# Half of the up-projection groups with tokens as rows, and all head pairs turned by DMA, in a two-layer decoder trunk

## The chip, the core and the metric

The kernel runs on one core of one Trainium2 chip. A core has TensorE (PE in the profile; PEld is its loading of the stationary operand), VectorE (DVE), ScalarE (ACT), GpSimd (POOL) and SyncE (SP), whose queue here issues nearly all DMAs. The metric is the device time of one execution in microseconds. Three runs of the kernel before took 555.38, 555.40 and 556.26 us, a median of 555.4.

## The reference

`x` is 256 tokens of 1024 features in fp32. There are two layers. Layer 0 mixes tokens with a gated MLP in chunks of 128 tokens, layer 1 with causal attention of 16 heads of 64 (with 256 tokens there is only the query's own block) and a relative-position bias. Each mixer is followed by a gated MLP with a causal depthwise convolution, and each of the four sub-layers ends in `x = LayerNorm(alpha * x + f(x))`:

```python
def conv_ffn(x, w_up, conv_w, conv_b, w_down):
    h = x @ w_up                                  # 1024 -> 2 x 2816
    hp = jnp.pad(h, ((0, 0), (CONV_WIDTH - 1, 0), (0, 0)))
    hc = conv_b
    for j in range(CONV_WIDTH):                   # width 3, along the tokens
        hc = hc + conv_w[j] * hp[:, j:j + S]
    g, val = jnp.split(hc, 2, axis=-1)
    return (jax.nn.gelu(g) * val) @ w_down

s = q k^T / 8 + bias[bucket(distance)]            # attention, causal
o = softmax(s) v
```

## The kernel before, in words

**Precision.** Every large matmul is done in three: weights and activations are each split into a high part (rounded to fp32r) and a low part (the rest), and high x high, high x low and low x high are added in PSUM. Weights come as chunks of 128 x 2048 fp32 (1 MB) into one of two `raw` buffers by SP's queue (L407). ScalarE writes the high part `whi` (L383), VectorE the low part `wlo` (L389), each 128 x 1024 half into the next of ten buffers. So a chunk is loaded and split up to two and a half groups ahead of its use.

**Column form of the up stages.** `conv_up` makes 22 tiles of 128 gate features and 22 of 128 value features. A group takes two of each, 512 features in all, from two chunks. In the column form (`cols_apart`) a block of weights is the stationary operand and the tokens stream: per feature tile and block of 128 inputs one matmul of 512 columns (high weights against high and low tokens of all 256) and one of 256 (low weights against high tokens). All high parts of a group come first, then all low ones. The result has features as rows, as the convolution along the tokens wants it. Behind the first group of a stage (the head, below) ten such groups follow, counted from 0; the even ones use the four single banks (`bank`), the odd ones the two double ones (`twos`).

**Row form.** The first group of each up stage (the head) is made otherwise: the tokens are the stationary operand and 512 features of weights stream, three matmuls of 512 columns per block of inputs and half of the tokens. The result has tokens as rows and has to be turned. ScalarE copies the bank into two planes of 16-bit halves (`over`, L963), a DMA transposes them (`xbar`, L426, on SP's queue), and copies put the halves together again (`join`, L971 on VectorE, L973 on ScalarE).

**Gate.** `gate` convolves the four tiles (ScalarE one step, VectorE two each, L393), applies the GELU, multiplies and splits the product into the two parts that the down stage reads from `rr`. The down stage (`project_out`) is in row form, goes through the 22 feature tiles in order and takes the last six behind all others.

**Attention.** `project` makes queries and keys of a pair of heads in column form, `scores` the scores of two pairs (four heads) into both double banks. `softmax` reduces on VectorE (L1104), takes the exponential on ScalarE (L383) and normalises on VectorE (L1112). The probabilities must be turned before they meet the values. For pairs 0 to 5 this is done by DMA (`turn_apart`: copies into planes L1127, transpose L426, joins L1130); for pairs 6 and 7 by 12 transposes on TensorE through the identity (L377) and four copies out of PSUM on ScalarE (`take`). `apply` multiplies with the values; `values` makes the second half of the values behind the last scores.

**What sets the order.** All operations are recorded with a duration that the author estimates; a list scheduler (`Plan`) then places them, engine by engine, by due times worked back from TensorE's stream, and the order on each engine is fixed when the program is built. Matmuls of the main stream keep their recorded order; transposes, scores and applications are fillers that go in where the plan has them ready. The plan is made, VectorE's work just ahead of the first normalisation is held behind it, and the plan is made again.

Of the kernel before, what the change touches and what calls it, by code (L numbers as in the profile page):

```python
# [19 lines left out]
P = 128  # L20
# [34 lines left out]
PASSES = 1  # L55
# [3 lines left out]
LAST_TURN = (6,)  # L59
APART_BY = ['act/dve', 'act/dve', 'act/dve', 'act/dve', 'act/dve', 'act/dve', 'act/dve', 'act/dve']  # L60
JOINED_BY = ['dve/act', 'dve/act', 'dve/act', 'dve/act', 'dve/act', 'dve/act', 'dve/act', 'dve/act']
BY_XBAR = (0, 1, 2, 3, 4, 5)
# [29 lines left out]
class Plan:  # L92
# [44 lines left out]
    def emit(self):  # L137
        ops = self.ops
        for o in ops:
            for b in o.bufs:  # L140
                for q in b.prev:
                    o.deps.update(x for x in q.ops if x is not o)
            assert all(d.i < o.i for d in o.deps), "a group waits for one recorded after it"

        self.dues()
        order = self.schedule()
        first = [o for o in order if o.first]
        for o in order:
            if o.eng == "dve" and not o.first and first[0].start - LEAD <= o.start < first[0].start:
                o.after = first[-1]  # L150
        for _ in range(PASSES):
            self.dues()
            order = self.schedule()

        done, held = set(), []
        for o in order:
            held.append(o)
            while True:
                x = next((x for x in held if x.deps <= done and (x.after is None or x.after in done)), None)
                if x is None:  # L160
                    break
                held.remove(x)
                x.emit()
                done.add(x)
        assert not held
# [104 lines left out]
def trunk_kernel(ctx: ExitStack, tc: tile.TileContext, a: dict, out: bass.AP):  # L270
# [88 lines left out]
    def mms(seq, r, w, fill=False, into=None, ready=False, share=1, turn=0.0):  # L359

        ns = 0.0
        for o, l, x, _, _ in seq:
            n = flat(x)
            ns += (max(n, 240) + 32) / 2.4 * 0.96 if l.dtype == F32R else (218.0 if n <= P else n / 0.6 + 5)
# [400 lines left out]
    def project_out(name, nk, at, xold, li, rows_i):  # L765
# [7 lines left out]
        if name == "b_o":  # L773
            free[1:3] = free[2:0:-1]
# [145 lines left out]
    def conv_up(layer, h, l):  # L920
# [39 lines left out]
        def over(t, b, to):  # L960
            a = planes.new()
            av = a.ap.bitcast(U16)
            plan.op("act", 1040, lambda: nc.scalar.copy(av.rearrange("p (h x) -> p h x", h=2), halves(b.ap)), [b], [a])  # L963
            xbar(to.ap.bitcast(U16).rearrange("p (g t q) -> p t g q", t=NT, q=P)[:, t], av, [a], [(to, [t])])

        def join(to, o, j, by):
# [3 lines left out]
            if by == "dve":  # L970
                dve(440, lambda: nc.vector.tensor_copy(to_, src), [(to, range(NT))], part)  # L971
            else:
                plan.op("act", 770, lambda: nc.scalar.copy(to_, src), [(to, range(NT))], part)  # L973
# [16 lines left out]
        for i in range(2):  # L990
            o = oring.new()
            gate(i, [join(across, o, 2 * i + j, "act" if j in BY_ACT else "dve") for j in range(2)], psum=False)
        for n, i in enumerate(range(2, FT, 2)):
            subs = [sub(name, i + x, j) for x in range(2) for j in range(2)]
# [6 lines left out]
            for x in range(2):  # L1001
                spent(name, i + x)
                gate(i + x, joined(bs[x]) if n % 2 else joined_apart(bs[2 * x:2 * x + 2]), psum=False)
        return lambda k, t: (av[:, k, t * P:(t + 1) * P], lv[:, k, t * P:(t + 1) * P], [(ah, [k]), (al, [k])])


    def moba(h, l, scr):
# [108 lines left out]
        def by(engines, first, j, fn, r, w):  # L1116
            e = engines.split("/")[j % len(engines.split("/"))]
            ns = {"act": (860, 1080), "dve": (590, 620), "pool": (1050, 1050)}[e][not first]
# [59 lines left out]
        for i in range(PAIRS):  # L1178
# [4 lines left out]
            if i in TURNS_BEHIND:  # L1183
                turn(TURNS_BEHIND[i], end)
        visit(PAIRS - 2)(end)
        values(1, [bank(True) for _ in range(NT)], [(t, range(KT)) for t in range(NT)])
# [38 lines left out]
def _layout(i):  # L1225
# [32 lines left out]
    for n in range(DEPTH):  # L1258
        pairs = paired(up[n][:, :FFN], up[n][:, FFN:])
        head = pairs[:2].reshape(2, P, 2, KT, P).transpose(1, 3, 0, 2, 4)  # L1260
        pairs[:2] = head.reshape(P, 2, CH).transpose(1, 0, 2)
# [33 lines left out]
```

## Time and profile before

| | |
|---|---|
| profiled execution | 555.37 us, span 553.6 us, granted clock 0.997 |
| busy: PE, PEld, DVE, ACT | 546.0, 467.9, 477.8, 381.4 us |
| layer 0: mixer until about 88 us, up stage to 199, down stage 199 to 272 (by the chain) | |
| layer 1: attention from 272 and its output projection, until about 376; up stage 376 to 487, down stage from 487 | |
| DMA | 114.37 MB, mean 207 GB/s, 58.6% of 16 engines for the main queue |

The stages overlap where a normalisation lets the next one begin. A row of the chain of waits gives start, length, engine, tile, line and count of instructions; a row of the order of time gives start, busy time, engine, line, operation, tiles and shape; a row of groups ends in busy time, mean nanoseconds of one, and the idle time before them.

### The profile page before, as it was taken

Reading aid. Unit: us, or ns where it says so; the run is one execution under the profiler, and the core shown is the slowest. Engines: PE = TensorE matmul, PEld = TensorE weight load, DVE = VectorE, ACT = ScalarE, POOL = GpSimd, SP = SyncE. Lnnn points to the kernel's source line nnn. Section 1 sums busy time; section 2 is a strip of 40 time slices with the busy share of each in tenths; the row PEclk is TensorE's granted clock in tenths of the full one; section 3 lists DMA queues with packets and bytes.
Section 4 is the critical chain, followed back from the end, with each engine's and each line's share of the span. In section 5 each row is a group of like instructions: output and inputs, shape, how many; then the busy total and the mean of one; then the engine's idle time right before and its main releaser. Section 6 shows DMA issues by size and latency. Waiting matters only on the chain.

```text
span 553.6 us, 8263 instructions
## 1 busy us (share of the span) xinstructions
PE 546.0 (99%) x2990; PEld 467.9 (85%) x2990; DVE 477.8 (86%) x914; ACT 381.4 (69%) x708; POOL 16.5 (3%) x22
## 2 busy tenths in 40 slices
PE   9999999999999999999999999999999999999995
PEld 6889888988898888888888887888888988888885
DVE  5898989899999999568978998789899999899837
ACT  6657567977677777355668998487975777768711
POOL 0200210000000000001000000000000000000001
PEclk9999999999999999999999999999999999999998
DMA  8988418764555276753566886729744654465502
GB/s 322 418 307 326 160 76 200 299 224 153 190 206 194 95 247 227 287 206 146 176 220 144 197 244 235 286 94 281 272 157 167 218 220 153 153 255 207 223 0 76
DMA packets 33200, 114.37 MB, mean 207 GB/s; under 512 B 15926, under 2 KB 19208, under 8 KB 21000
## 3 DMA queue, kind: packets, MB, share of 16 engines
q1 hardware_dynamic: 32872, 113.59, 58.6%
q8 instruction: 23, 0.38, 0.3%
q10 hardware_dynamic: 288, 0.26, 0.1%
q14 instruction: 17, 0.14, 0.1%
HBM read 109.36 MB, written 1.07 MB: 199 GB/s over the span
## 4 chain that ended last, share of the span: by engine, by line
PE 92%; DVE 5%; DMA 2%; issue 0%; ACT 0%; POOL 0%; DVEq 0%; ACTq 0%
PE bank L371 60%; PE twos L371 30%; DVE wlo L389 2%; DMA raw<-in_a_out 1%; PE bank L377 1%; DVE x L393 1%; DMA ff<-in_head 1%; DVE stat L628 0%; DVE ff L389 0%; DVE ff L393 0%; DVE rr L389 0%; PE twos L377 0%; ACT whi L383 0%; POOL stat L634 0%; DVE stat L668 0%
## 5 line engine op out<-in xcount | busy, mean ns | idle before, releaser
L389 DVE TENSOR_TENSOR wlo<-raw,whi 128x1024 fp32r<-128x1024 f32 (+1 forms) x202 | 219.4, 1115 | 16.1 <-ACT whi L383 15.6
L383 ACT ACTIVATE whi<-raw 128x1024 fp32r<-128x1024 f32 (+1 forms) x202 | 186.1, 966 | 43.7 <-DMA raw<-in_f_up 15.3
L371 PE MATMUL bank<-whi,rr 128*128 128x512 f32 x432 | 134.7, 390 | 0.0
L371 PE MATMUL bank<-xt,whi 128*128 128x512 f32 x512 | 120.1, 390 | 0.0
L371 PEld LDWEIGHTS bank<-xt,whi 128*128 128x128 f32 x512 | 95.0, 188 | 19.0
L371 PEld LDWEIGHTS bank<-whi,rr 128*128 128x128 f32 x432 | 81.1, 188 | 17.3 <-issue 0.3
L371 PE MATMUL bank<-wlo,rr 128*128 128x512 f32 x216 | 84.1, 389 | 0.0
L393 DVE SCALAR_TENSOR_TENSOR ff<-ff,convc 128x255 f32<-128x255 f32 (+1 forms) x176 | 76.6, 477 | 7.1 <-ACT ff L383 6.7
L371 PE MATMUL twos<-xt,whi 128*128 128x512 f32 x320 | 74.4, 390 | 0.0
L371 PEld LDWEIGHTS twos<-xt,whi 128*128 128x128 f32 x320 | 59.4, 188 | 11.9
L371 PEld LDWEIGHTS bank<-xt,wlo 128*128 128x128 f32 x512 | 63.9, 191 | 1.8 <-issue 0.2
L371 PE MATMUL bank<-xt,wlo 128*128 128x256 f32 x512 | 65.3, 284 | 0.0
L383 ACT ACTIVATE ff<-ff,convc 128x256 f32<-128x256 f32 x88 | 48.6, 591 | 4.2 <-DVE ff L389 4.0
L371 PEld LDWEIGHTS bank<-wlo,rr 128*128 128x128 f32 x216 | 40.6, 188 | 8.1
L383 ACT ACTIVATE ff<-bank 128x256 f32<-128x256 f32 (+1 forms) x60 | 23.2, 391 | 29.7 <-PE bank L371 23.3
L371 PEld LDWEIGHTS twos<-xt,wlo 128*128 128x128 f32 x320 | 39.7, 192 | 0.8
L371 PE MATMUL twos<-xt,wlo 128*128 128x256 f32 x320 | 40.0, 283 | 0.0
L383 ACT ACTIVATE ff<-bank,lncol 128x128 f32<-128x128 f32 x48 | 18.8, 460 | 19.5 <-PE bank L377 19.4
L371 PE MATMUL twos<-whi,xt 128*128 128x512 f32 x96 | 31.4, 395 | 0.0
L371 PE MATMUL bank<-whi,xt 128*128 128x512 f32 x96 | 29.1, 393 | 0.4 <-DVE whi L414 0.4
L383 ACT ACTIVATE ff<-ff 128x256 f32<-128x256 f32 x52 | 19.9, 410 | 10.4 <-DVE rr L389 8.6
L383 ACT ACTIVATE ff<-twos 128x512 f32<-128x512 f32 (+1 forms) x24 | 13.4, 574 | 18.9 <-PE twos L371 17.2
(118 smaller groups left out, 532.1 us busy)
## 6 DMA issues: line engine op xcount, KB each, us to landing
raw<-in_f_up SPq DMA_DIRECT2D x44, 1024.0 KB, 4.8
raw<-in_f_dn SPq DMA_DIRECT2D x22, 1024.0 KB, 4.8
raw<-in_b_qk SPq DMA_DIRECT2D x8, 1024.0 KB, 4.8
lnrow<-in_lnrow SPq DMA_DIRECT2D x5, 1024.0 KB, 7.1
raw<-in_a_out SPq DMA_DIRECT2D x4, 1024.0 KB, 6.3
raw<-in_b_v SPq DMA_DIRECT2D x4, 1024.0 KB, 4.8
raw<-in_b_o SPq DMA_DIRECT2D x4, 1024.0 KB, 4.9
raw<-in_a_u SPq DMA_DIRECT2D x3, 1024.0 KB, 8.4
```

The source lines that it names most:

```text
L371: nc.tensor.matmul(o, l, x, start=start, stop=stop)
L377: nc.tensor.transpose(o, x, ident.ap)
L383: return plan.op("act", ns, lambda: nc.scalar.activation(o, x, func, **kw), r, w, table=table)
L389: return dve(70 + 1.04 * flat(x), lambda: nc.vector.tensor_tensor(o, x, y, op=op), r, w)
L393: lambda: nc.vector.scalar_tensor_tensor(o, x, s, y, op0=op0, op1=op1), r, w)
```

## The change

1. Groups 1, 3, 5 and 7 behind the head of each up stage (`ROWS`; the groups that used the double banks, except the last) are made in row form and turned by DMA as the head is: per group two `over`, two transposes, four joins, two of these on ScalarE (`LATE_BY_ACT`) and two on VectorE. Their gates are recorded behind those of the next group. The weights of these groups are laid out by rows on the host.
2. Pairs 6 and 7 are turned by DMA as the other pairs are (`BY_XBAR`, `LAST_TURN`).
3. The plan: estimates for copies and for wide matmuls are changed, the plan is made three times instead of twice, and the hold ahead of the first normalisation is renewed each time. Two banks of the attention's output projection are no longer swapped, and the banks of the last values are taken ahead of the last scores.

```diff
--- before.py
+++ after.py
@@ -52,14 +52,16 @@
 SOON = 5000.0
 LEAD = 1700.0
 WARM = 9
-PASSES = 1
+PASSES = 2
+ROWS = (1, 3, 5, 7), (1, 3, 5, 7)
+LATE_BY_ACT = (0, 1)
 ALSO = {4: (0, 1), 6: (2, 3)}
 TURNS = {}
 TURNS_BEHIND = {}
-LAST_TURN = (6,)
+LAST_TURN = ()
 APART_BY = ['act/dve', 'act/dve', 'act/dve', 'act/dve', 'act/dve', 'act/dve', 'act/dve', 'act/dve']
 JOINED_BY = ['dve/act', 'dve/act', 'dve/act', 'dve/act', 'dve/act', 'dve/act', 'dve/act', 'dve/act']
-BY_XBAR = (0, 1, 2, 3, 4, 5)
+BY_XBAR = (0, 1, 2, 3, 4, 5, 6, 7)
 BY_ACT = 0, 1
 
 
@@ -142,15 +144,13 @@
                     o.deps.update(x for x in q.ops if x is not o)
             assert all(d.i < o.i for d in o.deps), "a group waits for one recorded after it"
 
-        self.dues()
-        order = self.schedule()
-        first = [o for o in order if o.first]
-        for o in order:
-            if o.eng == "dve" and not o.first and first[0].start - LEAD <= o.start < first[0].start:
-                o.after = first[-1]
-        for _ in range(PASSES):
+        for _ in range(PASSES + 1):
             self.dues()
             order = self.schedule()
+            first = [o for o in order if o.first]
+            for o in order:
+                if o.eng == "dve" and not o.first and first[0].start - LEAD <= o.start < first[0].start:
+                    o.after = first[-1]
 
         done, held = set(), []
         for o in order:
@@ -361,7 +361,7 @@
         ns = 0.0
         for o, l, x, _, _ in seq:
             n = flat(x)
-            ns += (max(n, 240) + 32) / 2.4 * 0.96 if l.dtype == F32R else (218.0 if n <= P else n / 0.6 + 5)
+            ns += (max(n, 240) + 32) / 2.4 * 0.97 if l.dtype == F32R else (218.0 if n <= P else n / 0.6 + 5)
 
         def emit():
             if into is not None and not ready:
@@ -770,8 +770,6 @@
 
 
         free = [bank(True) for _ in range(2 * NT)]
-        if name == "b_o":
-            free[1:3] = free[2:0:-1]
         pieces = [[(o, HALF, free[2 * t + o // HALF]) for o in (0, HALF)] for t in range(NT)]
         cuts = [[(0, HALF), (HALF, HALF)], [(0, HALF), (HALF + S, S + 2), (HALF, S)] if last else
                 [(0, HALF), (HALF, S), (HALF + S, S)]]
@@ -960,7 +958,7 @@
         def over(t, b, to):
             a = planes.new()
             av = a.ap.bitcast(U16)
-            plan.op("act", 1040, lambda: nc.scalar.copy(av.rearrange("p (h x) -> p h x", h=2), halves(b.ap)), [b], [a])
+            plan.op("act", 905, lambda: nc.scalar.copy(av.rearrange("p (h x) -> p h x", h=2), halves(b.ap)), [b], [a])
             xbar(to.ap.bitcast(U16).rearrange("p (g t q) -> p t g q", t=NT, q=P)[:, t], av, [a], [(to, [t])])
 
         def join(to, o, j, by):
@@ -968,9 +966,9 @@
             part = [(o, [j % 2])]
             to_ = halves(o.ap[:, j % 2 * S:(j % 2 + 1) * S])
             if by == "dve":
-                dve(440, lambda: nc.vector.tensor_copy(to_, src), [(to, range(NT))], part)
+                dve(350, lambda: nc.vector.tensor_copy(to_, src), [(to, range(NT))], part)
             else:
-                plan.op("act", 770, lambda: nc.scalar.copy(to_, src), [(to, range(NT))], part)
+                plan.op("act", 640, lambda: nc.scalar.copy(to_, src), [(to, range(NT))], part)
             return part[0], o.ap[:, j % 2 * S:(j % 2 + 1) * S]
 
         bs = [half() for _ in range(NT)]
@@ -990,7 +988,25 @@
         for i in range(2):
             o = oring.new()
             gate(i, [join(across, o, 2 * i + j, "act" if j in BY_ACT else "dve") for j in range(2)], psum=False)
+        behind = None
         for n, i in enumerate(range(2, FT, 2)):
+            if n in ROWS[layer]:
+                bs = [half() for _ in range(NT)]
+                for ks in (range(KT // 2), range(KT // 2, KT)):
+                    for t, b in enumerate(bs):
+                        for k in ks:
+                            hi, lo = sub(name, i + k // 4, k // 2 % 2)
+                            ns, parts = slice(k % 2 * HALF, (k % 2 + 1) * HALF), range(2 * (k % 2), 2 * (k % 2) + 2)
+                            hk, lk, r = xt_at(h, l)(k, t)
+                            mms([(b.ap, x, w.ap[:, ns], k == 0 and j == 0, k == KT - 1 and j == 2)
+                                 for j, (x, w) in enumerate([(hk, hi), (hk, lo), (lk, hi)])], r + [(hi, parts), (lo, parts)], [b])
+                        if t == NT - 1:
+                            spent(name, i + ks[0] // 4)
+                across = place("ff", 20 * S, 4 * S)
+                for t, b in enumerate(bs):
+                    over(t, b, across)
+                behind = i, across
+                continue
             subs = [sub(name, i + x, j) for x in range(2) for j in range(2)]
             if n % 2:
                 bs = [two_banks(x) for x in range(2)]
@@ -1001,6 +1017,12 @@
             for x in range(2):
                 spent(name, i + x)
                 gate(i + x, joined(bs[x]) if n % 2 else joined_apart(bs[2 * x:2 * x + 2]), psum=False)
+            if behind:
+                late, across = behind
+                for x in range(2):
+                    o = oring.new()
+                    gate(late + x, [join(across, o, 2 * x + j, "act" if 2 * x + j in LATE_BY_ACT else "dve") for j in range(2)], psum=False)
+                behind = None
         return lambda k, t: (av[:, k, t * P:(t + 1) * P], lv[:, k, t * P:(t + 1) * P], [(ah, [k]), (al, [k])])
 
 
@@ -1115,7 +1137,7 @@
 
         def by(engines, first, j, fn, r, w):
             e = engines.split("/")[j % len(engines.split("/"))]
-            ns = {"act": (860, 1080), "dve": (590, 620), "pool": (1050, 1050)}[e][not first]
+            ns = {"act": (735, 930), "dve": (470, 505), "pool": (1050, 1050)}[e][not first]
             f = {"act": nc.scalar.copy, "dve": nc.vector.tensor_copy, "pool": nc.gpsimd.tensor_copy}[e]
             plan.op(e, ns, lambda: fn(f), r, w)
 
@@ -1182,8 +1204,9 @@
             end = project(i)
             if i in TURNS_BEHIND:
                 turn(TURNS_BEHIND[i], end)
+        bs = [bank(True) for _ in range(NT)]
         visit(PAIRS - 2)(end)
-        values(1, [bank(True) for _ in range(NT)], [(t, range(KT)) for t in range(NT)])
+        values(1, bs, [(t, range(KT)) for t in range(NT)])
         for i in range(0, PAIRS, 2):
             if all((i, i + 1) != x for x in ALSO.values()):
                 o = None
@@ -1257,8 +1280,9 @@
     up, dn = np.asarray(i["f_w_up"]), np.asarray(i["f_w_down"])
     for n in range(DEPTH):
         pairs = paired(up[n][:, :FFN], up[n][:, FFN:])
-        head = pairs[:2].reshape(2, P, 2, KT, P).transpose(1, 3, 0, 2, 4)
-        pairs[:2] = head.reshape(P, 2, CH).transpose(1, 0, 2)
+        for at in (0, *(2 * x + 2 for x in ROWS[n])):
+            head = pairs[at:at + 2].reshape(2, P, 2, KT, P).transpose(1, 3, 0, 2, 4)
+            pairs[at:at + 2] = head.reshape(P, 2, CH).transpose(1, 0, 2)
         g[f"f_up{n}"] = pairs
         g[f"f_dn{n}"] = by_rows(dn[n])
     mg, mb, fg, fb = (np.asarray(i[k]) for k in ("ln_mix_g", "ln_mix_b", "ln_ffn_g", "ln_ffn_b"))
```

**TensorE, group 1 of the up stage in layer 0.** `twos` are the double banks, `xt` the split tokens; a row gives out<-moving,stationary operand, and xN its number in a run. Before:

```order
L371 MATMUL twos_106<-xt,whi_67 128x512 x8
L371 MATMUL twos_106<-xt,whi_68 128x512 x8
L371 MATMUL twos_107<-xt,whi_69 128x512 x8
L371 MATMUL twos_107<-xt,whi_70 128x512 x8
L371 MATMUL twos_106<-xt,wlo_77 128x256 x8
L371 MATMUL twos_106<-xt,wlo_78 128x256 x8
L371 MATMUL twos_107<-xt,wlo_79 128x256 x8
L371 MATMUL twos_107<-xt,wlo_80 128x256 x8
```

Now, the first two weight blocks with the first 128 tokens, and the start of the same with the second 128:

```order
L371 MATMUL twos_106<-whi_67,xt 128x512
L371 MATMUL twos_106<-wlo_77,xt 128x512
L371 MATMUL twos_106<-whi_67,xt 128x512 x2
L371 MATMUL twos_106<-wlo_77,xt 128x512
L371 MATMUL twos_106<-whi_67,xt 128x512
L371 MATMUL twos_106<-whi_68,xt 128x512
L371 MATMUL twos_106<-wlo_78,xt 128x512
L371 MATMUL twos_106<-whi_68,xt 128x512 x2
L371 MATMUL twos_106<-wlo_78,xt 128x512
L371 MATMUL twos_106<-whi_68,xt 128x512
L371 MATMUL twos_107<-whi_67,xt 128x512
L371 MATMUL twos_107<-wlo_77,xt 128x512
```

Where eight blocks of eight matmuls stood, all with high weights ahead of all with low ones, there are now 48 matmuls of 512 columns, in which each high part is used next to its low part from the start of the group.

**SP's queue in the up stage of layer 0**, from the head on (- before, + now; `raw` the two weight buffers, `ff` the planes):

```order
 L407 DMA raw_85<-in_f_up 128x2048
 L407 DMA raw_86<-in_f_up 128x2048
-L407 DMA lnrow_91<-in_lnrow 128x2048
+L426 DMA_TRANSPOSE ff<-ff 128x8x128
 L407 DMA raw_85<-in_f_up 128x2048
+L426 DMA_TRANSPOSE ff<-ff 128x8x128
+L407 DMA raw_86<-in_f_up 128x2048
+L407 DMA raw_85<-in_f_up 128x2048
+L407 DMA raw_86<-in_f_up 128x2048
+L407 DMA raw_85<-in_f_up 128x2048
```

Two transposes now stand among the weight loads for each row group.

**TensorE at the end of the attention** (`ident` the identity, `lnrow` the values, `rr` the attention's output, `ff` the probabilities). Before:

```order
L371 MATMUL bank_110<-whi_70,rr 128x512
L371 MATMUL bank_110<-wlo_80,rr 128x512
L371 MATMUL bank_110<-whi_70,rr 128x512
L377 MATMUL twos_107<-ident,ff 128x128 x3
L377 MATMUL twos_106<-ident,ff 128x128 x3
L377 MATMUL twos_107<-ident,ff 128x128 x3
L377 MATMUL twos_106<-ident,ff 128x128 x3
L371 MATMUL bank_109<-whi_69,rr 128x512
L371 MATMUL bank_109<-wlo_79,rr 128x512
L371 MATMUL bank_109<-whi_69,rr 128x512
L371 MATMUL bank_111<-whi_69,rr 128x512
L371 MATMUL bank_111<-wlo_79,rr 128x512
```

Now, around the application of pairs 6 and 7 to the values:

```order
L371 MATMUL bank_110<-whi_70,rr 128x512
L371 MATMUL bank_111<-whi_70,rr 128x512
L371 MATMUL bank_111<-wlo_80,rr 128x512
L371 MATMUL bank_111<-whi_70,rr 128x512
L371 MATMUL twos_107<-ff,lnrow_91 64x256 x2
L371 MATMUL twos_107<-ff,lnrow_91 64x128 x2
L371 MATMUL twos_107<-ff,lnrow_91 64x256 x2
L371 MATMUL twos_107<-ff,lnrow_91 64x128 x2
L371 MATMUL bank_108<-whi_71,rr 128x512
L371 MATMUL bank_108<-wlo_81,rr 128x512
L371 MATMUL bank_108<-whi_71,rr 128x512
L371 MATMUL bank_109<-whi_71,rr 128x512
```

The 12 transposes are gone (each row stands for three), and the application of pairs 6 and 7 follows the first two blocks of the output projection; between it and the scores of these pairs stand the applications of pairs 2 and 3 and of 4 and 5, and 54 matmuls of 512 columns.

## The prediction

> **What bounds the kernel now.** I read the page first (busy time, then the chain of work that ended last), then TensorE's own waits, then the stages by windows.
>
> ```profile
> span 553.6 us, 8263 instructions
> PE 546.0 (99%) x2990; PEld 467.9 (85%) x2990; DVE 477.8 (86%) x914; ACT 381.4 (69%) x708; POOL 16.5 (3%) x22
> PE 92%; DVE 5%; DMA 2%; issue 0%; ACT 0%; POOL 0%; DVEq 0%; ACTq 0%
> ```
>
> Who waited for whom, on TensorE alone (us in all, times, longest):
>
> ```profile
> PE twos L1212 <- PEq L1288: 0.8, 1, 0.8
> PE bank L371 <- DVE whi L414: 0.4, 1, 0.4
> PE bank L377 <- DVE x L396: 0.3, 1, 0.3
> ```
>
> TensorE waits 0.8 us and 0.4 us at the start and 0.3 us once more in 553.6 us. Its busy time is modelled, so I checked the chain (start, length, what; an extract):
>
> ```profile
> 70.84 1.11 PE bank L377 x8
> ...
> 165.83 11.11 PE twos L371 x64
> ...
> 325.76 1.35 PE twos L371 x20
> 327.11 11.20 PE bank L371 x58
> 338.31 1.45 PE twos L371 x16
> ...
> 341.35 1.31 PE twos L377 x12
> ...
> 345.41 1.45 PE twos L371 x16
> ...
> 487.45 51.72 PE bank L371 x228
> ...
> 539.20 0.70 DVE x L393
> ```
>
> From 71 us to 539 us the chain never leaves TensorE's stream: each matmul starts when the one ahead of it lets it. So a matmul taken out is worth its full spacing, and a wait put in costs its full length. What follows 539 us (the closing normalisation on VectorE) hangs on the stream's end and moves with it. In the middle of an up stage (window from 132.50 to 154.70: PE, PEld, DVE, ACT, POOL; clock; DMA share; GB/s), VectorE is nearly as full, ScalarE and the DMA engines are not:
>
> ```profile
> 132.50:154.70 22.20, 22.20 (x129) 19.66 (x129) 20.97 (x38) 16.38 (x31) 0.00 (x0) 1.00 0.49 181
> ```
>
> **The change part by part.** The sum is made against the profiled execution's 555.37 us, which is the median of the runs shown (555.4); it lies 1.8 us over its span, and nothing in the change touches that remainder.
>
> *Row groups.* Eight groups (four in each up stage) of 64 matmuls become 48. The columns streamed are the same: 32 x 512 + 32 x 256 = 24,576 before, 48 x 512 = 24,576 after. So only a cost per matmul can be saved. The last down stage has 228 matmuls of 512 columns in 51.72 us, 226.8 ns each. A group of 64 takes 11.11 us; less 32 x 226.8 ns it leaves 120.4 ns for a 256-column one. Twice 120.4 less 226.8 is 14.0 ns that does not go with columns. A row group should take 48 x 226.8 ns = 10.89 us, 0.22 us less, and eight of them **1.8 us less**. The weight loads fall in number too and stay under the matmuls.
>
> *Head pairs 6 and 7.* The 12 transposes through the identity go from TensorE's stream: 1.31 us in the chain. The four copies that fetched them from PSUM go from ScalarE. **1.3 us less.**
>
> *Work added off TensorE.* The groups' rows, nearest in shape to what comes and goes (from the page, the window's order of time and the lines' own views):
>
> ```profile
> L383 ACT ACTIVATE ff<-twos 128x512 f32<-128x512 f32 (+1 forms) x24 | 13.4, 574 | 18.9 <-PE twos L371 17.2
> 112.61 0.69 DVE L389 TENSOR_TENSOR ff<-twos,ff 128x512 f32<-128x512 f32 x1
> L963 ACT COPY ff<-twos x4: 1006/1008/1012, 86.9 to 376.4; 128x1024 uint16<-128x1024 uint16 x4
> L973 ACT COPY ff<-ff x8: 762/766/779, 97.6 to 387.5; 128x512 uint16<-128x512 uint16 x8
> L1130 DVE COPY ff<-apart x3: 603/604/615, 305.2 to 330.6; 128x768 uint16<-128x768 uint16 x3
> ```
>
> Per row group ScalarE loses two copies of 0.57 and gains two of 1.01 and two of 0.77: +2.4 us. VectorE loses two additions of 0.69 and gains two copies of 128x512, which no row shows; between two thirds of 0.60 (by size) and all of it, so 0.40 to 0.60 each: it gains 0.2 to 0.6 us of air. Over a pair of groups (now about 22.0 us) ScalarE goes from 16.4 to 18.8 us busy, VectorE from 21.0 to about 20.5. Both still fit, so I cost this work at nothing. The cover is the lead of the weights, next. The gates' results are read only by the down stage's later feature tiles; moving them a group later costs nothing there.
>
> *The queue of loads.* Each row group puts two transposes on SP's queue between the weight loads, and a load behind a transpose waits until ScalarE has copied the bank. Rows for one load and its two conversions, and for the transposes of the up stages (issue time min/median/max):
>
> ```profile
> L389 DVE TENSOR_TENSOR wlo<-raw,whi 128x1024 fp32r<-128x1024 f32 (+1 forms) x202 | 219.4, 1115 | 16.1 <-ACT whi L383 15.6
> L383 ACT ACTIVATE whi<-raw 128x1024 fp32r<-128x1024 f32 (+1 forms) x202 | 186.1, 966 | 43.7 <-DMA raw<-in_f_up 15.3
> raw<-in_f_up SPq DMA_DIRECT2D x44, 1024.0 KB, 4.8
> L426 SPq DMA_TRANSPOSE ff<-ff x4: 1339/2232/3794, 88.7 to 377.4; - x4
> 159.96 1.22 DVE L389 TENSOR_TENSOR wlo<-raw,whi 128x1024 fp32r<-128x1024 f32 x1
> ```
>
> A chunk holds one of two buffers for 4.8 us of load, 2 x 0.97 of high parts and the last low parts of 2 x 1.12: about 9 us, so two buffers deliver a chunk every 4.5 us, 18 us for the four chunks of a pair of groups that lasts 22. Some 4 us are spare, against two transposes of 2.2 us at the median. Beside that there is the lead. A column group needs its low parts only after its 32 wide matmuls, 7.3 us in; a row group needs the first at once and the second 6 matmuls (1.4 us) behind its start. The shortest lead I found: the second low part of the group that starts at 165.83 is written by 161.18 (the last row above) and would be needed at 167.2: 6.0 us still. I take **0** for this part, bounded by 0 (the lead holds) and the second rival below.
>
> *The wait at pairs 6 and 7.* In the new order TensorE has this between the end of the scores of 6 and 7 and applying them: applying pairs 2 and 3 and pairs 4 and 5 (1.45 us each) and 54 matmuls of 512 columns (12.25): 15.1 us of cover. Behind the waiting instruction stand all remaining steps of the attention's output projection. On ScalarE the joins that wait for the transposes stand ahead of the projection's next weights. What has to happen inside it, by the rows of the same chain before (VectorE, then ScalarE in order of time, then DMA landings):
>
> ```profile
> 325.41 0.47 DVE L1112 TENSOR_SCALAR ff<-ff,smax 128x128 f32<-128x128 f32 x2
> 329.01 0.41 DVE L1104 CUSTOM_DVE_ANT_0 ff<-twos,ff 128x256 f32<-128x256 f32 x1
> 335.80 1.18 DVE L1112 TENSOR_SCALAR ff<-ff,smax 128x256 f32<-128x256 f32 x5
> 329.50 0.51 ACT L383 ACTIVATE ff<-ff,smax 128x256 f32<-128x256 f32 x1
> 330.87 1.06 ACT L1130 COPY ff<-apart 128x768 uint16<-128x768 uint16 x1
> 332.76 1.08 ACT L1130 COPY ff<-raw 128x768 uint16<-128x768 uint16 x1
> 325.65 0.83 ACT L1127 COPY raw<-ff 128x768 uint16<-128x768 uint16 x1
> apart<-apart SPq DMA_TRANSPOSE x3, 3.8
> raw<-raw SPq DMA_TRANSPOSE x3, 4.4
> ```
>
> Three exponentials fit between 329.50 and 330.87, 0.46 us each; in the new order all eight stand together: 3.7 us, begun 0.4 us after the first reduction. Then come the two joins of pairs 4 and 5 (1.06 + 1.08), the two copies (0.8 each), the second transpose (4.4) and its join (1.08): 0.4 + 3.7 + 2.1 + 1.6 + 4.4 + 1.1 = 13.3 us from the first reduction. That one came 1.9 us after the scores before (327.11 to 329.01), with two weight conversions ahead of it; now there is one, and I put it at 0.5: ready at 13.8, 1.3 us inside the cover. The far bound is the measured chain: pair 7's last normalisation ended 9.9 us after its scores (335.80 + 1.18 less 327.11), and pairs 4 and 5 took 8.0 us from theirs (325.41 + 0.47) to the last join (332.76 + 1.08): 17.8, a wait of 2.7 us. I take **0.3 us**, nearer to the sum since the interleaved work that makes up the difference stands elsewhere in the new order.
>
> Sum: 555.37 - 1.8 - 1.3 + 0.3 = **552.6 us**.
>
> **The rivals.** *The transposes of pairs 6 and 7 come back as a wait.* The chain runs as measured (17.8) and TensorE stands 2.7 us: 555.0 us, no change; a transpose landing beside a load could add to it. For it: three pairs of heads show such chains. Against it: those ran between projections that shared VectorE and ScalarE. The Trainium skill (VectorE: DVE Perf Modes, Rules for kernel authors) advises TensorE for a 128x128 transpose where PSUM will do as the target, and the DMA crossbar otherwise; by that rule this part should lose, which is this rival. The trace so far shows only pairs with more cover than these.
>
> *The weights come late in the up stages*, which ends on the slower side. Mechanism: a transpose on SP's queue waits for the bank copy and then holds the queue, so both raw buffers stand empty. Let a row group hold it for h in all. A stage then loses four times what h has over the 4 us spare, less the 6.0 us of lead: 4 (h - 4) - 6.0, in each of two stages. The gain begins to go at h = 5.5 us, and from h = 6.0 (8 x 2.0 - 12 = 4.0 us lost, 3.1 won) the kernel is slower than before. At 6.2 it is 552.6 + 8 x 2.2 - 12 = 558.2 us; at twice the longest issue, 7.6, it would be 569. Against it: the pairs of transposes before cost no wait on TensorE, and 2 x 2.2 is under 5.5.
>
> *Nothing per matmul is saved.* If the 14 ns belong to the short matmuls' form, time goes with columns and 24,576 take 11.11 us either way: 552.6 + 1.8 = 554.4 us. Against it: 48 per group is just the rate of the 228 quoted. The Trainium skill (TensorE: Matmul & The Clock Gate, Back-to-back issue gap) gives N/2.4 + 2.5 ns for one matmul on its own, 16 x 2.5 ns = 0.04 us a group and an estimated 0.3 us in all in place of 1.8; this trace's 226.8 and 120.4 ns fit a fixed part of 14 ns, not 2.5.
>
> **How the numbers follow.** The forecast holds with 0.61 (552.1 to 553.4, from waits of 0 to 1 us and moved transposes of the normalisations, some 0.2 us either way); the wait at pairs 6 and 7 0.18 (553.4 to 556); late weights 0.14 (554 and up); nothing per matmul 0.05; the rest 0.02. A measurement of this kernel can tell about 0.2%, 1.1 us, from no change. Faster by more (under 554.3): 0.61 + a third of the wait's 0.18 + half of the 0.05 = 0.70. Within: 0.08 of the wait, 0.03 of late weights, the rest: 0.15. Slower: 0.15. The range runs from 551.9 (both savings, no wait, 0.6 us from the moved work) to 555.7, which leaves out most of the late weights and the worst wait: 2 in 10.
>
> **What would show it.** Row groups right: the chain shows 48 in 10.9 us where 64 took 11.1; wrong: 11.1, or TensorE waits on weight conversions in them. Pairs 6 and 7 right: no L377 group of 12, and TensorE waits under 1 us for a join ahead of the last application; wrong: a wait of 2 us or more there. Queue right: raw loads still land in about 5 us and the low parts lead by over 3 us in row groups. The prediction falls if TensorE's busy share drops below 98% of its span.

## The result, and the profile after

The changed kernel takes 552.25 us (median of 6 runs, 551.75 to 553.39) against 555.50 us for the kernel before on the same chip: a ratio of 0.9937, 95% interval 0.9926 to 0.9949. The forecast was 552.6. The profiled execution took 552.33 us with a span of 550.6, 3.0 us less than the 553.6 before.

From the page of the changed kernel: span, busy times, and the share of each engine in the chain that ended last. Under it, TensorE's only wait (us in all, times, longest).

```profile
span 550.6 us, 8040 instructions
PE 543.5 (99%) x2850; PEld 460.0 (84%) x2850; DVE 472.1 (86%) x918; ACT 399.6 (73%) x724; POOL 16.3 (3%) x22
PE 96%; DVE 2%; DMA 1%; issue 0%; ACT 0%; SPq 0%; DVEq 0%; ACTq 0%
```
```profile
PE twos L1235 <- PEq L1312: 0.8, 1, 0.8
```

140 matmuls and transposes are gone from TensorE, and the one wait that the profile still names is the one at the start of the program, which stood there before too. ScalarE is 18 us busier and VectorE 6 us less, and TensorE waits for neither. The chain of the changed kernel (start, length, what; an extract) says which stages got shorter:

```profile
88.11 11.09 PE bank L371 x64
99.20 10.91 PE twos L371 x48
110.11 11.09 PE bank L371 x64
...
198.29 27.23 PE bank L371 x120
...
286.38 1.35 PE twos L371 x20
...
327.70 10.52 PE bank L371 x55
338.22 1.45 PE twos L371 x16
339.67 3.62 PE bank L371 x15
343.29 1.45 PE twos L371 x16
344.74 12.46 PE bank L371 x54
...
374.29 11.09 PE bank L371 x64
...
484.46 51.72 PE bank L371 x228
```

The same chain of the kernel before, an extract:

```profile
88.06 11.09 PE bank L371 x64
...
199.17 27.25 PE bank L371 x120
...
287.17 1.35 PE twos L371 x20
...
376.35 11.09 PE bank L371 x64
```

The first up stage behind its head group runs from 88.11 to 198.29, 110.18 us; the second from 374.29 to 484.46, 110.17 us. The kernel before has the same stages from 88.06 to 199.17 and from 376.35 to 487.45, 111.11 and 111.10 us. That is 1.86 us. The stretch from the first block of scores (286.38) to the end of the last application (344.74) takes 58.36 us, before 59.69 (287.17 to 346.86): 1.33 us, the 12 transposes. The other stages differ by 0.1 us or less each. 1.86 + 1.33 less 0.2 is the 3.0 us of the span.

### The profile page after: what moved, and what is told of

It is laid out like the page before. It is cut to its first block, busy times and chain, and to the rows that moved or that the text cites. A ratio compares the mean times of both kernels' runs of the same rounds, so it can differ in the third digit from the quotient of the medians.

```text
span 550.6 us, 8040 instructions
## 1 busy us (share of the span) xinstructions
PE 543.5 (99%) x2850; PEld 460.0 (84%) x2850; DVE 472.1 (86%) x918; ACT 399.6 (73%) x724; POOL 16.3 (3%) x22
## 3 DMA queue, kind: packets, MB, share of 16 engines
q1 hardware_dynamic: 52904, 118.57, 64.6%
HBM read 109.36 MB, written 1.07 MB: 201 GB/s over the span
## 4 chain that ended last, share of the span: by engine, by line
PE 96%; DVE 2%; DMA 1%; issue 0%; ACT 0%; SPq 0%; DVEq 0%; ACTq 0%
PE bank L371 64%; PE twos L371 30%; DMA ff<-in_head 1%; PE bank L377 1%; DVE x L393 1%; DVE ff L393 0%; SPq L407 0%; DVE stat L628 0%; ACT whi L383 0%; DVE stat L668 0%; DVE ff L671 0%; DVE x L389 0%; DVEq L1315 0%; DVE x L671 0%; DVE x L687 0%
## 5 line engine op out<-in xcount | busy, mean ns | idle before, releaser
L371 PE MATMUL twos<-whi,xt 128*128 128x512 f32 x352 | 111.9, 391 | 0.0
L371 PEld LDWEIGHTS twos<-whi,xt 128*128 128x128 f32 x352 | 66.1, 188 | 13.3
L371 PE MATMUL twos<-wlo,xt 128*128 128x512 f32 x176 | 68.6, 390 | 0.0
L383 ACT ACTIVATE ff<-ff,convc 128x256 f32<-128x256 f32 x88 | 50.0, 595 | 5.9 <-DVE ff L389 5.4
L371 PEld LDWEIGHTS twos<-wlo,xt 128*128 128x128 f32 x176 | 33.1, 188 | 6.2
L393 DVE SCALAR_TENSOR_TENSOR x<-x,bank 128x512 f32<-128x512 f32 x16 | 10.9, 683 | 21.9 <-PE bank L371 21.9
L634 POOL TENSOR_TENSOR stat<-stat,nhalf 128x1 f32<-128x1 f32 x9 | 9.0, 1000 | 479.0 <-DVE stat L633 479.0
```

The costliest lines, as they stand in the source:

```text
L371: nc.tensor.matmul(o, l, x, start=start, stop=stop)
L383: return plan.op("act", ns, lambda: nc.scalar.activation(o, x, func, **kw), r, w, table=table)
L393: lambda: nc.vector.scalar_tensor_tensor(o, x, s, y, op0=op0, op1=op1), r, w)
L634: plan.op("pool", 700, lambda: nc.gpsimd.tensor_tensor(rstd, ve, nhalf.ap, op=ALU.pow), [(st, ["ve"]), nhalf], [(st, ["rstd"])])
```

## The experiments

**Which part brings what.** Three kernels take the change apart: row groups alone, pairs alone, and neither (only the planner's numbers, passes and bank order).

```
rows_only    -BY_XBAR = (0, 1, 2, 3, 4, 5, 6, 7)          +BY_XBAR = (0, 1, 2, 3, 4, 5)
             -LAST_TURN = ()                              +LAST_TURN = (6,)
pairs_only   -ROWS = (1, 3, 5, 7), (1, 3, 5, 7)           +ROWS = (), ()
plan_only    all three lines
```

> The changed kernel without its second part: head pairs 6 and 7 go back to the 12 transposes on TensorE; row groups and the new planner numbers stay. By my sum this keeps 8 x 0.22 = 1.8 us: 553.6 us against 555.4 before. The changed kernel's chain showed 0.20 us per row group and some 0.03 us per column group beside it: 1.86 in all, 553.5. Rival (gain comes from the planner's new numbers, not the groups): same as before, 555.4, with the groups still at 11.1 us.

> The changed kernel without row groups; head pairs 6 and 7 still turned by DMA, planner numbers new. My theory: 1.3 us less than before, 554.1 us, and no wait of TensorE ahead of applying pairs 6 and 7 (the wait of 0.3 us in my sum did not show in the changed kernel). Rival (the transposes come back as a wait of up to 2.7 us once the rest of the order is as before): 555.4 or more, with TensorE waiting for a join.

> Only the planner's part: new cost estimates, a second pass, the banks of the attention's projection in their plain order; no row groups, pairs 6 and 7 on TensorE as before. My theory: 0, that is 555.4 within 0.3 us, since TensorE's stream has the same instructions and hardly waits. Rival (the plan itself brings part of the 3 us): 1 us or more faster than before.

| kernel | median us | ratio to the kernel before | 95% interval |
|---|---|---|---|
| rows_only | 553.65 | 0.9966 | 0.9954 to 0.9978 |
| pairs_only | 554.39 | 0.9977 | 0.9969 to 0.9986 |
| plan_only | 555.39 | 0.9998 | 0.9990 to 1.0007 |
| both (the change) | 552.25 | 0.9937 | 0.9926 to 0.9949 |

Times 555.4, the ratios are 1.9, 1.3 and 0.1 us; they add up to 3.3, and the change has 3.5 (2.8 to 4.1). Within these intervals the parts add up, and the planner's new numbers by themselves bring nothing that can be measured. All three went as my theory had it.

**What a matmul costs beside its columns.** The row groups stream the same columns through more matmuls: in the first up stage the third product of each three is cut in two, in the second every matmul of a group is cut but the first one of each half of the tokens.

```
-mms([(b.ap, x, w.ap[:, ns], ...) for j, (x, w) in enumerate(...)], ...)
+mms([(b.ap[:, c:c + n_], x, w.ap[:, ns][:, c:c + n_], ...) for j, (x, w) in enumerate(...)
+     for n_ in (S if j == 2 or layer == 1 and k + j else HALF,) for c in range(0, HALF, n_)], ...)
```

> The changed kernel with the same columns streamed by more matmuls in the row groups: in the first up stage each matmul of the low part of the tokens is cut in two of 256 columns (64 per group in place of 48), in the second up stage all but the first are cut (95 per group). Theory of the prediction (14.0 ns per matmul that does not go with columns): 16 x 14 ns = 0.22 us per group in the first stage, which brings its groups back to the 11.1 us of the column form, 47 x 14 ns = 0.66 us in the second; 4 x 0.22 + 4 x 0.66 = 3.5 us more than the changed kernel, 555.8 us. Rival (time goes with columns, and the row form gained by something else): 552.3 us, groups at 10.9. Rival (the weight loads, 161 ns each by the page's busy time over their count, set the pace of 256-column matmuls): 95 x 161 ns = 15.3 us per group in the second stage, 17 us more in all.

555.94 us, ratio 1.0000 (0.9991 to 1.0009); by the ratios that is 3.5 us over the changed kernel, as expected. Its chain shows a row group of each stage:

```profile
99.24 11.15 PE twos L371 x64
...
386.44 11.51 PE twos L371 x94
```

In the first stage 16 matmuls more cost 0.24 us (11.15 less 10.91), 15 ns each. In the second, 46 more cost 0.60 us, 13 ns each. (The expectation counted 95 matmuls a group; the edit leaves two uncut, so 94 is right.) Sixty-four matmuls in row form take what sixty-four take in column form, so the gain is the count and not the form. The rival by which time goes with columns alone has fallen; so has the one on weight loads, which wanted 15.3 us for a group.

**A doubled transpose for pair 7.**

```
-xbar(bv..., av, [(a, [0, 1])], [b])
+xbar(bv..., av, [(a, [0, 1])], [b], times=2 if i == PAIRS - 1 else 1)
```

> The changed kernel with the transpose of head pair 7 issued twice, the second after the first has landed (4.4 us later), with the same result. Theory: in the changed kernel the last join was done 14.0 us after the scores and its reader came 15.6 us after them, so 1.6 us of the delay are covered and the rest is a wait: 4.4 - 1.6 = 2.8 us more than the changed kernel, 555.1 us, seen as one wait of TensorE for a join, of that length. Rival (the cover is larger than the chain shows, because other work of TensorE can step in): 552.3 us.

554.81 us, ratio 0.9986 (0.9977 to 0.9995): 2.6 us over the changed kernel, near the expected 2.8, but not as one wait. SP's queue and TensorE's instructions in order of time (start, length, what), first as the change has them, then with the repeat:

```profile
333.96 1.44 SPq L426 DMA_TRANSPOSE apart<-apart  x1
335.51 1.74 SPq L426 DMA_TRANSPOSE raw<-raw  x1
337.35 2.02 SPq L407 DMA_DIRECT2D raw<-in_b_o  x2
...
340.26 1.07 ACT L1152 COPY ff<-raw 128x768 uint16<-128x768 uint16 x1
341.08 0.60 DVE L1152 COPY ff<-raw 128x768 uint16<-128x768 uint16 x1
```
```profile
340.17 1.42 SPq L428 DMA_TRANSPOSE raw<-raw  x1
341.69 1.44 SPq L407 DMA_DIRECT2D raw<-in_b_o  x2
...
345.00 1.37 PE L371 MATMUL twos<-ff,lnrow 128*64 128x256 f32 x8 [0.25 <-DVE ff L1155]
```

In the changed kernel the last join ends at 341.68, 14.0 us after the scores (327.70), and the application starts at 343.29, 15.6 us after them. Its first eight matmuls belong to pair 6, so pair 7, whose join is the last, has some 0.7 us more (half of the 1.45). With the repeat these eight run on time, and TensorE stands only 0.25 us for the join ahead of the eight of pair 7, which then take 1.37 us where all sixteen took 1.5 in the changed kernel. From the end of the scores to the end of the application it loses 1.0 us (18.0 in place of 17.0). The projection's 54 matmuls behind it then lose 0.9 us more (346.30 to 359.73, 13.4 in place of 12.5): the loads of the projection's weights left the queue at 341.69 in place of 337.35, 4.3 us later, behind the repeat. That makes 1.9 us for the repeat; in this execution 0.65 us more lie ahead of the scores, at 327 us, which the repeat can't have caused. So the expected 2.8 us was too much, and the agreement of the medians is partly chance. A late transpose is paid partly on the queue, by late weights, which the expectation left out. The margin is real, and for pair 7 it is some 2.3 us, not the 1.6 of the expectation.

**SP's queue held for longer.** The row groups' transposes are issued twice, the second ones of a group in the first up stage, both in the second.

```
-xbar(to..., av, [a], [(to, [t])])
+xbar(to..., av, [a], [(to, [t])], times=2 if t or layer else 1)
```

> The changed kernel with transposes of the row groups (and of the head group) issued twice, the second after the first has landed, both with the same result: in the first up stage only the second of a group's two transposes, in the second up stage both. A repeat holds SP's queue for one landing (4.2 us) and one more issue (1.3). Held per row group: 1.3 + 5.5 + 1.3 = about 7 to 8 us less the first issue counted once, say 6.8, in the first stage, 11.0 in the second. By the formula of the prediction's second rival (spare 4 us per pair of groups, lead 6.0 us): 4 x 2.8 - 6.0 = 5.2 us lost in the first stage and 4 x 7.0 - 6.0 = 22 in the second, about 579 us. By the changed kernel's own leads (least lead 7.6 us, growing by 2.7 us per pair of groups with 3.3 us of transposes on the queue, so 6.0 us spare): nothing in the first stage, 4 x 5.0 - 7.6 = 12 us in the second, about 565 us. If SP's queue does not matter at all: 552.3 us, no wait of TensorE.

585.62 us, ratio 1.0542 (1.0527 to 1.0558), more than any theory had. The three transposes of one row group of the first stage, as the queue issued them, then TensorE's waits:

```profile
142.30 6.75 SPq L428 DMA_TRANSPOSE ff<-ff  x3
```
```profile
PE bank L371 <- DVE ff L389: 10.2, 2, 5.8
PE twos L371 <- ACT ff L964: 7.9, 2, 7.3
PE bank L371 <- ACT whi L383: 2.0, 1, 2.0
PE twos L615 <- DVE cast L603: 1.8, 1, 1.8
```

The queue was held for 6.75 us, as reckoned (6.8). In the first up stage TensorE did not stop until 187 us, and then for 0.6 us and for a bank. The loss came behind it: the down stage stood from 200.30 to 205.05 for gated features, since ScalarE had waited 3.5 us for a load with a step of the gate behind it in its order, and VectorE with it. In the second layer the stops (2.4, 7.6 and 6.2 us, each with the matmul before it) were for weights, for a bank that ScalarE had not copied, and, in the down stage, for features again. And the stops cost more than their length. Windows of the same execution, a stop and what follows it, two times (from:to, length, busy PE, PEld, DVE, ACT, POOL, granted clock, DMA share, GB/s):

```profile
200.30:205.05 4.75, 0.35 (x2) 0.00 (x0) 1.78 (x5) 3.50 (x7) 0.00 (x0) 0.91 0.66 266
205.05:210.76 5.71, 5.71 (x13) 4.51 (x14) 5.71 (x9) 5.54 (x10) 0.00 (x0) 0.50 0.10 16
210.76:215.00 4.24, 4.24 (x19) 3.51 (x18) 3.96 (x11) 2.38 (x5) 0.00 (x0) 0.97 0.95 386
463.90:471.49 7.59, 0.28 (x4) 0.08 (x2) 4.39 (x8) 6.08 (x10) 0.00 (x0) 0.71 0.75 276
471.49:477.20 5.71, 5.71 (x13) 4.46 (x14) 5.57 (x12) 5.54 (x9) 0.00 (x0) 0.50 0.64 208
```

Thirteen matmuls take 5.71 us at a clock of 0.50, 0.44 us each, where the stream else takes 0.227: 2.8 us on top of each stop, three times, 8.3 us in all. The formula of the prediction gave 579 us without this. It was near for the wrong reasons: the queue can be held longer than 6 us before weights are late, but ScalarE's and VectorE's other work is late before them.

**The gates a group later, or at once.** The group's joins and gates are recorded right behind its transposes.

```
-behind = i, across
+for x in range(2):
+    o = oring.new()
+    gate(i + x, [join(across, o, 2 * x + j, ...) for j in range(2)], psum=False)
```

> The changed kernel with a row group's joins and gates recorded right behind its transposes in place of one group later. Theory (nothing on TensorE reads the gates before the down stage, and ScalarE and VectorE are ordered by due times anyway): no difference, 552.3 us, no stop of TensorE. Rival (the delay is needed: joins that wait for a transpose of 3 to 8 us stand in ScalarE's and VectorE's order ahead of weight conversions, and bank copies come late): TensorE stops in the up stages, 1 us or more slower than the changed kernel.

552.55 us, ratio 0.9939 (0.9926 to 0.9952), with no wait of TensorE in the up stages: the delay brings nothing that can be measured and costs nothing. The order on ScalarE and VectorE does change; TensorE does not feel it.

**More row groups.** If every row group is worth 0.2 us, why not all ten? The gates then follow a group later, and the turned planes alternate between two places. In this and the next four kernels work that has come due is also recorded inside row groups (`plan.tick()`), which the changed kernel does not do; what that does by itself was not run.

```
-ROWS = (1, 3, 5, 7), (1, 3, 5, 7)
+ROWS = tuple(range(10)), tuple(range(10))
-across = place("ff", 20 * S, 4 * S)
+across = place("ff", (20 if n % 2 else 10) * S, 4 * S)
```

> The changed kernel with all ten groups of each up stage behind the head in row form (20 in place of 8), each gated a group later, their turned planes in two places by turns. Theory that only the count of matmuls sets the time: 12 groups more at 0.18 to 0.22 us each, 2.2 to 2.6 us less than the changed kernel: 549.7 to 550.1. Rival by my formula for SP's queue: two transposes per group hold it for about 6.6 us per pair of groups, 2.6 over the 4 us spare, 4 x 2.6 - 6.0 = 4.4 us lost in each of two stages: about 558.5. Rival ScalarE: it was busy 19.9 of 22.0 us per pair of groups in the changed kernel and gets 2.4 us more, 22.3 of 21.8; the low lead of 7.6 us covers four such shortfalls of 0.5 us: no wait, but the leads shrink through the stage where they grew before.

554.85 us, ratio 0.9985 (0.9970 to 1.0000), and executions from 553.1 to 557.7: worse than eight row groups. TensorE's waits, then the first eleven microseconds of the first up stage as a window:

```profile
PE twos L371 <- ACT ff L961: 2.5, 3, 1.0
```
```profile
89.40:100.40 11.00, 10.90 (x48) 8.52 (x47) 7.29 (x11) 6.24 (x9) 0.00 (x0) 1.00 1.07 307
```

The span is 553.0 us where 550.6 less 2.2 was due: 4.6 us are lost, in nine short stops of TensorE's stream from the head to the fourth group of both stages. The waits that the profile names, 2.5 us in three stops, are for banks that ScalarE has not copied. The DMA engines are full there (a share of 1.07 by the records), but that alone stops nothing: in the first column group of the stage the changed kernel has 1.05 and the kernel before 1.03, and TensorE runs through. What differs is that with all rows the share stays high (1.16 in the next 11 us, where the changed kernel has 0.73). Two kernels leave the first even groups in column form:

```
rows_late    +ROWS = (1, 3, 5, 6, 7, 8, 9), (1, 3, 5, 6, 7, 8, 9)
rows_late8   +ROWS = (1, 3, 4, 5, 6, 7, 8, 9), (1, 3, 4, 5, 6, 7, 8, 9)
```

> Row form for groups 1, 3, 5, 6, 7, 8, 9 of each up stage (14 in place of 8). With all twenty, TensorE stood still for 4.7 us, all of it in the first four groups of each stage and none later. Theory (the weights' lead is short only at a stage's start): 6 more groups at 0.18 to 0.20 us each, 1.1 us less than the changed kernel: 551.1 us, no stop of TensorE in the up stages. Rival (row groups one behind the other overload ScalarE, the queue or the DMA engines wherever they stand): stops again, 552.3 us or more.

> As the run before with group 4 in row form too (16 groups). If the lead at group 3 is enough, 1.5 us less than the changed kernel, 550.8 us. If three row groups in a row from group 3 run into the stage's start, stops of 0.5 to 2 us in each stage as with all twenty: 551.5 to 554.

553.31 us, ratio 0.9963 (0.9942 to 0.9984), and 552.40 us, ratio 0.9939 (0.9927 to 0.9951). My theory that the stops belong to the stage's start fell: in rows_late the first stage has none, but the second has two at its end. In rows_late8 likewise: no named wait in the first stage, two in the second (1.0 us, at 418 and at 476), again for bank copies; its 552.40 is inside the range that its expectation gave for stops. ScalarE's order of time at the two stops of rows_late, then the matmuls that waited:

```profile
469.48 2.02 ACT L383 ACTIVATE whi<-raw 128x1024 fp32r<-128x1024 f32 x2 [2.00 <-DMA raw<-in_f_dn]
...
472.19 0.99 ACT L961 COPY ff<-twos 128x1024 uint16<-128x1024 uint16 x1
...
475.66 0.99 ACT L961 COPY ff<-twos 128x1024 uint16<-128x1024 uint16 x1
```
```profile
473.24 0.50 PE L371 MATMUL twos<-whi,xt 128*128 128x512 f32 x1 [0.69 <-ACT ff L961]
...
476.70 0.50 PE L371 MATMUL twos<-whi,xt 128*128 128x512 f32 x1 [0.44 <-ACT ff L961]
```

ScalarE stands 2.0 us for a load of the next stage's weights, with the bank copy behind it in its order, and TensorE stands with it (473.24). Row groups one behind the other share four halves of two double banks. By the kernel's own bookkeeping, from which the plan is made, a group takes halves that the group before the last has left. The trace shows a shorter leash: the two copies are those of group 8, and the two halves of the tokens of group 9, the group right behind it, start some 0.05 us after each of them ends. By the bookkeeping group 9 writes the halves that group 8 did not, so its matmuls waited for a copy out of the other half of their double bank; why was not looked into. Column groups used the four single banks in between, which now lie idle. So the last two kernels let even row groups accumulate there:

```
-bs = [half() for _ in range(NT)]
+bs = [half() if n % 2 else bank() for _ in range(NT)]
```

> Row groups 1, 3, 5, 6, 7, 8, 9 as before, but the even ones accumulate in the four single banks that the column groups used, so that a bank is wanted again after three groups in place of one. In the run without this, TensorE stopped twice for 1.5 us in all at the end of the second up stage for a bank that ScalarE had not copied yet, though the weights lay ready. Theory (the bank copies are the only thing late): no stop, 6 x 0.18 = 1.1 us less than the changed kernel, 551.1 us, and a spread like the changed kernel's. Rival (ScalarE is behind as a whole, so the stop moves to late weights or to late gates in the down stage): 552 us or more.

> All ten groups in row form, even ones in the single banks. The leads of the low parts with twenty row groups were 8.4 us and more except for the last group of the first stage (1.5 us), and every stop was for a bank. Theory (bank copies only): no stop, 12 x 0.18 = 2.2 us less than the changed kernel, 550.1 us. Rival (loads, transposes and ScalarE are behind as a whole at the stage's start): stops on late weights in the first groups or on late features in the down stage, 552 us or more.

With seven row groups per stage: 551.30 us (550.80 to 551.64), ratio 0.9916 (0.9903 to 0.9928). No stop in the up stages:

```profile
154.63 10.88 PE bank L371 x48
165.51 10.88 PE twos L371 x48
176.39 10.88 PE bank L371 x48
187.27 10.88 PE twos L371 x48
198.15 27.20 PE bank L371 x120
```

Both stages take 109.50 us in place of 110.18, 1.36 us less in all, and the bank copies were indeed the thing late in rows_late: the one edit between the two kernels takes the ratio from 0.9963 to 0.9916, and the intervals are apart. It is the fastest kernel of this study, about 1 us under the changed one (1.2 by the ratios); the two intervals just overlap, and the two were not timed side by side. With all ten: 553.07 us, ratio 0.9943 (0.9922 to 0.9964), executions from 550.7 to 555.8. The profiled execution, of 555.6 us, stops on late weights at the end of the first stage and, in the down stage, ahead of a normalisation's transposes:

```profile
PE bank L377 <- DVE x L396: 2.2, 1, 2.2
PE twos L371 <- DVE wlo L389: 1.4, 1, 1.4
```

That is the rival in the main, though its stops were expected in the first groups or on late features: with twenty row groups more than the bank copies is late in some executions. Which of the loads, the transposes, ScalarE and VectorE sets the limit was not separated, and this one execution alone was profiled.

## Why the prediction was right

*Row groups, 1.8 us.* Predicted 10.89 us for 48 matmuls, measured 10.91 next to column groups and 10.88 among row groups. Eight groups at 0.20 are 1.6; the column groups beside them fell from 11.11 to 11.09. In all 1.86 by the stages and 1.9 by the row groups alone. The step that carried it, a fixed 14.0 ns per matmul, came out at 13 to 15 ns in the split.

*Pairs 6 and 7, 1.3 us less and 0.3 us of wait.* The 1.3 stands (1.33 in the chain, 1.3 timed). The wait is the mis-sized term: it was 0. The chain of work was ready 14.0 us after the scores, against 13.8 in the sum; the cover was 15.6 us, against 15.1, since each block of small matmuls takes some 0.2 us longer than its row in the chain. I had the mechanism and then added 0.3 us out of caution. That the 13.8 fits so well is partly luck. The first reduction began 0.3 us before the scores ended, where the sum had 0.5 us behind them, and the second transpose landed at 339.49; but the two joins of pair 7 stood behind other work in the orders of ScalarE and VectorE and began only at 340.26 and 341.08, a delay that the sum did not have. The 0.3 us of wait is the difference between 552.6 and the profiled 552.33; 0.1 us more from the two savings and 0.2 us lost in the other stages nearly cancel beside it. By the Trainium skill (VectorE: DVE Perf Modes, Rules for kernel authors) TensorE should do a 128x128 transpose if PSUM will do as its target; here, with TensorE the bound and 15.6 us of cover, the measurement decides for the DMA by 1.3 us.

*Work off TensorE, nothing.* Right: the joins on VectorE take 0.46 us, inside the 0.40 to 0.60, and TensorE waited for no engine. ScalarE's load was sized too small: it was busy 19.7 to 20.1 us in a pair of groups of 22.0 (from 110.11 on), where the sum had 18.8; VectorE had 20.8 to 21.7, where the sum had 20.5. Both still fit. Rows of the changed kernel:

```profile
L969 DVE COPY ff<-ff x16: 451/458/469, 133.7 to 483.0; 128x512 uint16<-128x512 uint16 x16
```
```profile
raw<-in_f_up SPq DMA_DIRECT2D x44, 1024.0 KB, 5.2
```

*The queue, 0 us.* Loads land in 5.2 us at the median, in place of 4.8. The shortest lead in a row group is that of group 1 of the first stage (VectorE's writes of two low parts, then the first matmul that reads the earlier one):

```profile
95.93 2.36 DVE L389 TENSOR_TENSOR wlo<-raw,whi 128x1024 fp32r<-128x1024 f32 x2 [1.29 <-ACT whi L383]
```
```profile
104.73 0.39 PE L371 MATMUL twos<-wlo,xt 128*128 128x512 f32 x1
```

The earlier of the two is done by 97.2, 7.6 us before its use, and the leads grow to over 15 us by group 7. The price of 0 was right; the second rival's formula was not. Its spare of 4 us was too small, it took late weights to be the first thing to show, where in the run with doubled transposes late features and late bank copies cost most, and it lacked the half clock after a stop.

*The planner's numbers, nothing named.* 0.1 us by themselves, within their interval of no change.

*The rivals.* The wait at pairs 6 and 7 exists as a mechanism: one transpose more brings 1.9 us, half of it as late weights. The rival that nothing per matmul is saved fell by the split.

## What to carry to other kernels

Where TensorE is the bound and the stream is dense, price a change by the number of matmuls as well as by their columns: this kernel pays 13 to 15 ns for each. Work moved off TensorE cost nothing here while the cover, counted from the chain, exceeded the chain of work that must fit in it. Before adding more of it, ask which in-order engine holds the bank copies, and behind which load they stand. Letting row groups alternate between two sets of accumulator banks took away the stops that came with seven row groups per stage (553.3 to 551.3 us).

## What the hardware showed that was not expected

A stop of TensorE of 4.75 us or more was followed each time by 13 matmuls at half the granted clock (0.50 for 5.7 us), 2.8 us beyond the stop itself; stops of 2.2 us (233.61 to 235.79) and 2.4 us (431.96 to 434.39) in the same run were not. The Trainium skill (TensorE: Matmul & The Clock Gate, What's actually happening) says that the clock falls to half after an idle window of about 3.4 us and comes back after a busy one; the trace agrees on the fall, and the half clock lasted 5.7 us each time.

The transposes weigh on the DMA engines more than their bytes say. The queue line of the page, before and after:

```profile
q1 hardware_dynamic: 32872, 113.59, 58.6%
```
```profile
q1 hardware_dynamic: 52904, 118.57, 64.6%
```

The 18 added transposes move 5 MB in 20,000 packets. The share rises by 64.6% of 550.6 less 58.6% of 553.6, 31 us of all 16 engines. If all of it is theirs, that is 1.7 us per transpose and about 160 GB/s, where the queue before, with its ten transposes, ran at about 350. The packets of the changed kernel by size agree: those of 256 bytes, which are the 28 transposes, move 8.4 MB in 51.5 us of all 16 engines, 163 GB/s, and those of 8 KB run at 366.
